# Half-width filter loads with on-chip copies, two convolutions joined without a store, and the last output blocks of a hybrid encoder layer

## The chip, the cores and the metric

The kernel runs on one core of one Trainium2 chip. The metric is the device time of one execution in microseconds (us). A core has five engines with a queue each: TensorE (PE in the profile), VectorE (DVE), ScalarE (ACT), GpSimd (POOL) and SyncE (SP), which here only issues transfers. Each engine works through its own instructions in a fixed order and waits where an operand is not there yet.

## What is computed

One encoder layer on 2048 rows of 1024 channels, in float32. The parts that matter here are the long convolutions of the Hyena group (512 channels, order 2) and the end of the layer:

```python
for o, gate in enumerate((g1, g2)):
    conv = irfft(rfft(z, n=2 * L, axis=1) * spec[:, o], n=2 * L, axis=1)[:, :L]
    z = gate * (conv + z * skip[o])
...
h = h + square(relu(rms_norm(h, norm_ff_g) @ ff_w1)) @ ff_w2
return rms_norm(h, final_norm_g)
```

Beside the Hyena group stand an mLSTM group, cross-attention and the MLP; all of them start from large projections.

## The kernel before

**The order of the program.** The projections are products of 32-bit data split into a high and a low half (`mm3`, lines 336 to 338: three matmuls per tile). While the input projection runs (`sweep`, `natural`), the filter spectra are made (`filters`) and then the two convolutions (`hyena`); `weave` alternates between the Python generators by the cost that each `yield` names, and a scheduler then sets the order on each engine by its own model of time. After that come the mLSTM scan, attention, and the MLP (`ffn`).

**A convolution** is a Fourier transform of 4096 points in two stages of small matrices. For each order `o` (0 and 1) there are three phases. *Phase 1*, 8 steps: rows of `z` are loaded (`load1`), multiplied with `f1` (L863), copied out of PSUM and stored to `zs` in device memory. *Phase 2*, 16 steps: `load2` fetches the matrices `dm` and `em`, a transposed piece `t` of `zs`, and the filter's real and imaginary parts `hr` and `hi` from `hd`. The product with `dm` (L877) is multiplied with the complex filter on ACT (L879, L880: the two halves swapped, one negated), DVE (L881, L883) and POOL (L882), multiplied with `em` (L845), copied (L846) and stored to `zg`. As real and imaginary rows lie in partitions 0 to 63 and 64 to 127, `hr` and `hi` are needed twice each, in both halves, and are loaded twice (L818, L819). *Phase 3*, 8 steps: `load3` fetches `zg` and the gate, the product with `e2` (L896) is multiplied by the gate (L897). For order 0 the result is stored to `z1` (L899), from which phase 1 of order 1 loads it again. Large tiles of the convolution share one ring of 10 buffers (`ta`), and all their transfers are issued by SP.

**The end.** The MLP's second product runs as 28 products of halves, each in two column blocks `tp` with four steps `k` (12 matmuls of 128x512 a step). In the last seven (`o == 3`) finished blocks are turned: `turn` transposes four 128x128 tiles (L1653), ACT squares and sums them (L1655), DVE multiplies by the gain (L1656). `finish` combines two halves of sums into a row scale (`rsqrt`, ten small DVE instructions), multiplies 8 tiles by it (L1671 on DVE, L1673 on ACT) and stores them (L1677). These pieces wait in the list `outs`, from which one or two are taken in each step:

```python
for _ in range(min(len(outs), 2 if len(outs) > 5 else 1)):
    outs.pop(0)("mm" if tp else "hy")
```

What is left after the last step is emitted after it: with this rule two turns of block 0, its `finish`, four turns of block 2 and its `finish`.

Of the kernel before, what the change touches and what calls it, by code (L numbers as in the profile page):

```python
# [13 lines left out]
ALU = mybir.AluOpType  # L14
# [5 lines left out]
D = 1024  # L20
CH = 512
EPS = 1e-6
# [103 lines left out]
class Prog:  # L126
# [654 lines left out]
    def hyena(self, es):  # L781
# [4 lines left out]
        z1 = self.dram("z1", (128, 16, CH))  # L786
# [15 lines left out]
        def load1(o, j2):  # L802
            z = ta()
            js = slice(2 * j2, 2 * j2 + 2)
            nc.sync.dma_start(out=z, in_=hy[0, :, js] if o == 0 else z1[:, js])
# [43 lines left out]

        for o in range(2):  # L850
            sd, gd = sds[o], gds[o]
            q = [load1(o, 0), load1(o, 1)]
            for j2 in range(8):
                yield 3.5
                js = slice(2 * j2, 2 * j2 + 2)
                z = q.pop(0)
                if j2 < 6:
                    q.append(load1(o, j2 + 2))
                st = [ta() for p in range(2)]
                for jj in range(2):  # L860
                    for p in range(2):
                        pp = self.hy()
                        nc.tensor.matmul(pp, f1[:, p], z[:, jj], start=True, stop=True)  # L863
                        self.copy(st[p][:, jj], pp)
                for p in range(2):
                    nc.sync.dma_start(out=sd[p, :, js], in_=st[p])
            nxt = load2(o, 0)
            for i in range(16):
# [5 lines left out]
                gs = ta()  # L874
                for m in range(2):
# [11 lines left out]
            for j2 in range(8):  # L887
                yield 3.5
# [22 lines left out]
                nc.sync.dma_start(out=yh[:, js], in_=sq)  # L911

# [299 lines left out]
    def attention(self, es):  # L1212
# [64 lines left out]
        for c in range(4):  # L1277
# [129 lines left out]
            def stats(c=c, ssum=ssum):  # L1407
# [12 lines left out]
                nc.vector.reciprocal(rbp[:, 4 * c:4 * c + 4], rbp[:, 4 * c:4 * c + 4])  # L1420
# [89 lines left out]
    def ffn(self):  # L1510
# [115 lines left out]
        with tc.tile_pool(name="down", bufs=1) as B:  # L1626
# [31 lines left out]
            def finish(c, dst, last):  # L1658
                rb = self.rbp[:, 4 * c:4 * c + 4]
                m = B.tile([128, 4], F32, tag="mo", name="mo", bufs=2)  # L1660
                nc.vector.tensor_tensor(m, ss[:, c, 0], ss[:, c, 1], ALU.add)
                nc.vector.tensor_tensor(m, m, rb, ALU.mult)
                nc.vector.tensor_tensor(m, m, rb, ALU.mult)
                nc.vector.tensor_scalar(m, m, 1.0 / D, EPS, ALU.mult, ALU.add)
                rv = self.rsqrt(B, m, "or")
                nc.vector.tensor_tensor(rv, rv, rb, ALU.mult)
                for h in range(2):
                    for t in range(4):
                        v = dst[h][:, t]
                        if last and t % 2:  # L1670
# [3 lines left out]
                        if last and t % 2 or t == 3:  # L1674
                            n = 2 if last else 4
                            r0 = 512 * c + 128 * (t + 1 - n)
                            nc.sync.dma_start(  # L1677
                                out=self.out[r0:r0 + 128 * n, 512 * h:512 * h + 512].rearrange("(t p) c -> p t c", p=128),
                                in_=dst[h][:, t + 1 - n:t + 1])

            def turned(c, tp, h, i, j):
                return [lambda tag, t=t: turn(c, h, acc[i, tp], acc[j, tp], t, tag) for t in range(4)]
# [8 lines left out]
            for s, (n, tp, k) in enumerate(down):  # L1691
# [19 lines left out]
                for _ in range(min(len(outs), 2 if len(outs) > 5 else 1)):  # L1711
                    outs.pop(0)("mm" if tp else "hy")
                if k < 3:
                    continue
                for m in range(4):
# [3 lines left out]
                    else:  # L1719
                        nc.vector.tensor_tensor(v, bank[m], v, ALU.add)  # L1720
# [15 lines left out]
                elif i == 3:  # L1736
# [3 lines left out]
                    outs += turned(c, tp, 0, 3, 6)  # L1740
                    outs.append(lambda tag, c=c, d=(acc[6, tp], acc[1, tp]): finish(c, d, False))
                elif i == 2:
                    outs += turned(2 * tp, tp, 0, 2, 7)
                elif i == 4:
                    outs += turned(2 * tp, tp, 1, 4, 5)
                    outs.append(lambda tag, c=2 * tp, d=(acc[7, tp], acc[5, tp]), tp=tp: finish(c, d, tp))
# [108 lines left out]
```

## Time and profile before

| | |
|---|---|
| three runs | 3331.58, 3334.69, 3346.91 us; median 3334.69 |
| profiled execution | 3330.15 us, of which the span on the core 3328.4 us |
| PE busy | 3155.0 us, 95% of the span |
| DVE, ACT, POOL busy | 1975.6, 1473.0, 1253.8 us |
| data moved | 680.87 MB, mean 205 GB/s over the span |

PE is the engine that carries the span, so the question in each stretch is where PE stands still, or runs at a lower granted clock, and what ended last before it went on. A busy share near 1 of the DMA engines in a stretch says that the transfers themselves are the limit there. PE's busy time is a model: matmuls are pipelined, and the records of one overlap with the next.

### The profile page before, as it was taken

The page shows a single profiled execution, that of the slowest core. Times are in us where ns is not written, and L with a number is a line of the kernel's source. Part 1 is how long each engine was busy: PE and PEld are TensorE (multiplying, and loading weights), DVE is VectorE, ACT ScalarE, POOL GpSimd, SP SyncE. Part 2 cuts the span into 40 slices and gives each one's busy share as a digit, 9 for nine tenths or more (in the row PEclk, how much of TensorE's full clock was granted, in tenths as well). Part 3 has the DMA queues.
Part 4 walks back from the last instruction along what each step waited for, and adds up shares of the span by engine and source line. Part 5 has one row for each costly group of instructions (what it writes and reads, how often), then busy time and mean ns, then how long its engine had stood idle before and what let it go on. Part 6 is the DMA issues. An engine that isn't in the chain of part 4 may idle for free.

```text
span 3328.4 us, 45502 instructions
## 1 busy us (share of the span) xinstructions
PE 3155.0 (95%) x15293; PEld 2512.1 (75%) x15293; DVE 1975.6 (59%) x3312; ACT 1473.0 (44%) x2827; POOL 1253.8 (38%) x868
## 2 busy tenths in 40 slices
PE   7999999899999998699999998999999999999997
PEld 5655666576666887598888897888788887888876
DVE  7684324433555755676766565665754686565695
ACT  5442444542454244355454444555655543333335
POOL 0132000220122303634334115876765574434482
PEclk9999999999999999899999999999999999999998
DMA  5553897999998669858557525764644475444434
GB/s 177 178 195 134 291 310 248 281 267 347 247 270 272 220 214 301 273 155 249 177 186 237 188 95 185 227 204 161 223 163 152 158 238 167 130 139 143 127 93 160
DMA packets 483461, 680.87 MB, mean 205 GB/s; under 512 B 40816, under 2 KB 252912, under 8 KB 482204
## 3 DMA queue, kind: packets, MB, share of 16 engines
q1 hardware_dynamic: 482584, 676.04, 64.6%
q8 instruction: 121, 1.98, 0.2%
q0 software_dynamic: 496, 1.84, 0.2%
q14 instruction: 112, 0.92, 0.1%
q10 hardware_dynamic: 148, 0.10, 0.0%
HBM read 458.64 MB, written 219.18 MB: 204 GB/s over the span
## 4 chain that ended last, share of the span: by engine, by line
PE 72%; DMA 14%; DVE 5%; issue 3%; ACT 2%; POOL 2%; SPq 1%; ACTq 0%; DVEq 0%; POOLq 0%
PE mm L336 14%; PE mm L337 14%; PE mm L338 14%; PE hy L338 5%; PE hy L336 5%; PE hy L337 5%; DMA a<-hd 2%; PE hy L271 2%; PE hy L319 2%; PE hy L896 2%; DVE wl L341 1%; DMA rw<-rows 1%; PE hy L863 1%; PE mm L719 1%; PE hy L286 1%
## 5 line engine op out<-in xcount | busy, mean ns | idle before, releaser
L341 DVE TENSOR_TENSOR wl<-wn,wh 128x512 fp32r<-128x512 f32 (+1 forms) x364 | 290.8, 836 | 152.7 <-ACT wh L341 140.5
L1436 DVE TENSOR_TENSOR bl<-wr,bh 128x512 fp32r<-128x512 f32 x213 | 239.4, 1131 | 123.9 <-ACT bh L1435 121.5
L341 ACT CAST wh<-wn 128x512 fp32r<-128x512 f32 (+1 forms) x364 | 208.4, 618 | 230.8 <-DMA wn<-in_w_in_dram 79.8
L1435 ACT CAST ah<-w 128x512 fp32r<-128x512 f32 x284 | 176.1, 621 | 298.8 <-PE hy L337 152.1
L336 PE MATMUL mm<-xh,wh 128*128 128x512 f32 x640 | 280.3, 440 | 6.5 <-ACT P L685 2.9
L337 PE MATMUL mm<-xl,wh 128*128 128x512 f32 x640 | 276.4, 433 | 0.6 <-DVE xl L498 0.6
L338 PE MATMUL mm<-xh,wl 128*128 128x512 f32 x640 | 266.3, 417 | 0.0
L882 POOL TENSOR_TENSOR b<-b,a 128x512 f32<-128x512 f32 x64 | 88.8, 1390 | 466.2 <-DVE a L823 211.5
L1436 DVE TENSOR_TENSOR al<-w,ah 128x512 fp32r<-128x512 f32 x236 | 229.2, 973 | 58.6 <-ACT ah L1435 58.3
L1435 ACT CAST bh<-wr 128x512 fp32r<-128x512 f32 x232 | 143.3, 621 | 234.1 <-PE mm L338 171.4
L338 PE MATMUL mm<-bh,al 128*128 128x512 f32 x576 | 225.6, 394 | 7.7 <-DVE al L1436 4.9
L336 PE MATMUL mm<-bh,ah 128*128 128x512 f32 x576 | 227.2, 394 | 0.0
L337 PE MATMUL mm<-bl,ah 128*128 128x512 f32 x576 | 226.0, 392 | 0.0
L336 PE MATMUL mm<-act,wh 128*128 128x512 f32 x512 | 200.0, 394 | 0.9 <-ACT wh L341 0.9
L337 PE MATMUL mm<-act,wh 128*128 128x512 f32 x512 | 200.5, 392 | 0.0
L338 PE MATMUL mm<-act,wl 128*128 128x512 f32 x512 | 198.8, 392 | 0.0
L1293 POOL TENSOR_TENSOR ssum<-ssum,sq 128x512 f32<-128x512 f32 x56 | 80.7, 1441 | 278.8 <-ACT sq L1292 278.8
L336 PE MATMUL hy<-bh,ah 128*128 128x512 f32 x448 | 175.3, 392 | 0.0
L337 PE MATMUL hy<-bl,ah 128*128 128x512 f32 x448 | 174.8, 390 | 0.0
L338 PE MATMUL hy<-bh,al 128*128 128x512 f32 x448 | 174.7, 390 | 0.0
L295 POOL TENSOR_TENSOR b<-b 128x512 f32<-128x512 f32 x32 | 66.5, 2078 | 281.8 <-DVE b L290 147.9
L336 PEld LDWEIGHTS mm<-xh,wh 128*128 128x128 f32 x640 | 122.2, 191 | 64.0 <-issue 30.0
(365 smaller groups left out, 8861.3 us busy)
## 6 DMA issues: line engine op xcount, KB each, us to landing
wr<-hc SPq DMA_DIRECT2D x224, 256.0 KB
w<-in_ff_w_dram SPq DMA_DIRECT2D x176, 256.0 KB
a<-hd SPq DMA_DIRECT2D x128, 256.0 KB
hc<-t SPq DMA_DIRECT2D x128, 256.0 KB
wn<-in_w_in_dram SPq DMA_DIRECT2D x100, 256.0 KB
hc<-q SPq DMA_DIRECT2D x96, 256.0 KB
fs<-a SPq DMA_DIRECT2D x32, 512.0 KB
a<-fs SPq DMA_DIRECT2D x32, 512.0 KB
```

What stands on the lines that cost most here:

```text
L271: nc.tensor.matmul(pp, f1[:, p], e[p], start=True, stop=True)
L295: nc.gpsimd.tensor_tensor(e[1], f, b, ALU.subtract)
L319: nc.tensor.matmul(pp, dm[:, m], t[:, m], start=True, stop=True)
L336: mm(ps, lh, rh, start=start, stop=False)
L337: mm(ps, lh, rl, start=False, stop=False)
L338: mm(ps, ll, rh, start=False, stop=stop)
L341: both = (self.nc.scalar.copy(hi, src), self.nc.vector.tensor_tensor(lo, src, hi.bitcast(F32), ALU.subtract))
L882: nc.gpsimd.tensor_tensor(xt, xt, hi[:, m], ALU.mult)
L896: nc.tensor.matmul(pp, e2[:, p], r[p][:, jj], start=p == 0, stop=p == 1)
L1293: nc.gpsimd.tensor_tensor(ssum, ssum, sq, ALU.add)
L1435: self.nc.scalar.copy(hi, src)
L1436: eng.tensor_tensor(lo, src, hi.bitcast(F32), ALU.subtract)
```

## The change

There are four parts.

1. `load2` loads `hr` into partitions 0 to 63 and `hi` into 64 to 127 only. A new function `double` makes the other halves on the chip: ACT copies `hr` upward, DVE copies `hi` downward, 64 partitions by 1024 numbers each. For the first piece one row is set apart as before, now without a transfer.
2. Phase 3 of order 0 and phase 1 of order 1 are one loop. The gated result stays on the chip, and the function `spectrum` (phase 1 in a form for both orders) multiplies it with `f1` one step later; `z1` is gone. A step of this loop names a cost of 7.0 and no longer 3.5.
3. In the last product two pieces of `outs` are taken in each step, and `finish` is part of its block's last turn, so block 0 is done within the last product and only block 2 is left after it. All stores go out in pieces of 256 rows by 512 columns; most are issued by ACT, the others by SP. In blocks 0 and 2 one half is multiplied on DVE.
4. The row scale is worked out with fewer small instructions: `rbp` holds EPS times the square of the mean square, and `finish` needs two instructions ahead of `rsqrt` and none behind it.

```diff
         def load2(o, i):
...
-            for h in range(2):
-                nc.sync.dma_start(out=hr[64 * h:64 * h + 64], in_=src[0])
-                nc.sync.dma_start(out=hi[64 * h:64 * h + 64], in_=src[1])
+            nc.sync.dma_start(out=hr[0:64], in_=src[0])
+            nc.sync.dma_start(out=hi[64:128], in_=src[1])
+            return dm, em, t, hr, hi
+
+        def double(i, hr, hi):
+            nc.scalar.copy(hr[64:128], hr[0:64])
             if i == 0:
-                nc.sync.dma_start(out=hr[64:65, 0], in_=hd[o, 0, 64:65])
-                nc.vector.memset(hi[0:1, 0], 0.0)
+                nc.scalar.copy(hr[64:65, 0], hi[64:65, 0])
                 nc.vector.memset(hi[64:65, 0], 0.0)
-            return dm, em, t, hr, hi
+            nc.vector.tensor_copy(hi[0:64], hi[64:128])
...
+        def spectrum(o, j2, z):
+            st = [ta() for p in range(2)]
+            for jj in range(2):
+                for p in range(2):
+                    pp = self.hy()
+                    nc.tensor.matmul(pp, f1[:, p], z[:, jj], start=True, stop=True)
+                    self.copy(st[p][:, jj], pp)
+            for p in range(2):
+                nc.sync.dma_start(out=sds[o][p, :, 2 * j2:2 * j2 + 2], in_=st[p])
...
                 if i < 15:
                     nxt = load2(o, i + 1)
                 gs = ta()
+                double(i, hr, hi)
...
             for j2 in range(8):
-                yield 3.5
+                yield 3.5 if o else 7.0
...
                 if o == 0:
-                    nc.sync.dma_start(out=z1[:, js], in_=gate)
+                    late(lambda j2=j2, gate=gate: spectrum(1, j2, gate))
                     continue
...
+            late(None)
...
-                nc.vector.reciprocal(rbp[:, 4 * c:4 * c + 4], rbp[:, 4 * c:4 * c + 4])
+                nc.vector.scalar_tensor_tensor(rbp[:, 4 * c:4 * c + 4], rbp[:, 4 * c:4 * c + 4], EPS,
+                                               rbp[:, 4 * c:4 * c + 4], ALU.mult, ALU.mult)
...
-            def finish(c, dst, last):
-                rb = self.rbp[:, 4 * c:4 * c + 4]
+            def finish(c, dst):
                 m = B.tile([128, 4], F32, tag="mo", name="mo", bufs=2)
-                nc.vector.tensor_tensor(m, ss[:, c, 0], ss[:, c, 1], ALU.add)
-                nc.vector.tensor_tensor(m, m, rb, ALU.mult)
-                nc.vector.tensor_tensor(m, m, rb, ALU.mult)
-                nc.vector.tensor_scalar(m, m, 1.0 / D, EPS, ALU.mult, ALU.add)
+                q = self.rbp[:, 4 * c:4 * c + 4]
+                for h in range(2):
+                    nc.vector.scalar_tensor_tensor(m, ss[:, c, h], 1.0 / D, m if h else q, ALU.mult, ALU.add)
                 rv = self.rsqrt(B, m, "or")
-                nc.vector.tensor_tensor(rv, rv, rb, ALU.mult)
-                for h in range(2):
-                    for t in range(4):
+                for t in range(4):
+                    for h in range(2):
                         v = dst[h][:, t]
-                        if last and t % 2:
+                        if h and c % 2 == 0:
                             nc.vector.tensor_scalar(v, v, rv[:, t:t + 1], None, ALU.mult)
                         else:
                             nc.scalar.mul(v, v, rv[:, t:t + 1])
...
+                        if t % 2:
+                            r0 = 512 * c + 128 * (t - 1)
+                            (nc.sync if h and c % 2 == 0 else nc.scalar).dma_start(
...
-                for _ in range(min(len(outs), 2 if len(outs) > 5 else 1)):
+                for _ in range(min(len(outs), 2 if len(outs) > 4 or n + 1 == len(prods) else 1)):
                     outs.pop(0)("mm" if tp else "hy")
...
-                        nc.vector.tensor_tensor(v, bank[m], v, ALU.add)
+                        d = nc.vector.tensor_tensor(v, bank[m], v, ALU.add)
+                        if s + 1 == len(down):
+                            tc.keep_in_program_order(d)
```

The number of matmuls is the same. The order of the instructions differs in the convolutions' stretch and at the end; between them and ahead of them it is the same but for a few neighbours that changed places. Three places show it.

SP, phase 2 of order 0, the loads of one step: before, with `zs0` the transformed signal, `hd` the filter, `em` and `dm` the matrices and `zg0` the result.

```order
L815 DMA a_3907<-zs0_3223 128x2x512
L818 DMA a_3908<-hd_321 64x2x512
L819 DMA a_3909<-hd_321 64x2x512
L813 DMA em_3904<-in_c_em_dram 128x256
L818 DMA a_3908<-hd_321 64x2x512
L819 DMA a_3909<-hd_321 64x2x512
L848 DMA zg0_3225<-a_3821 128x2x512
L812 DMA dm_3973<-in_c_dm_dram 128x256
```

And the same step of the changed kernel on SP.

```order
L814 DMA a_3903<-zs0_3222 128x2x512
L816 DMA a_3904<-hd_321 64x2x512
L817 DMA a_3905<-hd_321 64x2x512
L812 DMA em_3900<-in_c_em_dram 128x256
L849 DMA zg0_3224<-a_3813 128x2x512
L811 DMA dm_3969<-in_c_dm_dram 128x256
```

Two of eight transfers of a step are gone; the others stand in the same order.

ACT in the same step: before, `b` is the swapped product, `P` a piece of the input projection that leaves PSUM, `a_3821` the result on its way to `zg`.

```order
L846 COPY a_3821<-hy_3840 128x512
L879 ACTIVATE b_3918<-hy_3916 64x512
L880 COPY b_3918<-hy_3916 64x512
L846 COPY a_3821<-hy_3925 128x512
L879 ACTIVATE b_3931<-hy_3929 64x512
L880 COPY b_3931<-hy_3929 64x512
L685 COPY P_4378<-mm_4487 128x512
```

And the changed kernel on ACT, where `a_3904` is the `hr` of the step after.

```order
L847 COPY a_3813<-hy_3836 128x512
L882 ACTIVATE b_3914<-hy_3912 64x512
L883 COPY b_3914<-hy_3912 64x512
L685 COPY P_4441<-mm_4416 128x512
L821 COPY a_3904<-a_3904 64x1024
L847 COPY a_3813<-hy_3921 128x512
L882 ACTIVATE b_3927<-hy_3925 64x512
L883 COPY b_3927<-hy_3925 64x512
L847 COPY a_3909<-hy_3934 128x512
```

The copy of `hr` stands between the other work of ACT, five instructions ahead of the step that uses it.

ACT at the end of the program, from the squares of the last turns on (`ss` the sums, `or_y` the row scale, `acc` the output tiles): before.

```order
L1655 ACTIVATE junk_29702,ss_24134<-mm_29697 128x512
L1655 ACTIVATE junk_29710,ss_24134<-mm_29705 128x512
L1655 ACTIVATE junk_29718,ss_24134<-mm_29713 128x512
L1655 ACTIVATE junk_29726,ss_24134<-mm_29721 128x512
L1673 ACTIVATE acc_24122<-acc_24122,or_y_29674 128x512 x4
L1673 ACTIVATE acc_24126<-acc_24126,or_y_29674 128x512 x4
L1673 ACTIVATE acc_24123<-acc_24123,or_y_29734 128x512 x2
L1673 ACTIVATE acc_24127<-acc_24127,or_y_29734 128x512 x2
```

And the changed kernel on ACT at its end.

```order
L1675 ACTIVATE acc_24095<-acc_24095,or_y_29615 128x512 x4
L1678 DMA out_0_dram<-acc_24095 128x2x512 x2
L1660 ACTIVATE junk_29672,ss_24107<-mm_29667 128x512
L1660 ACTIVATE junk_29680,ss_24107<-mm_29675 128x512
L1660 ACTIVATE junk_29688,ss_24107<-mm_29683 128x512
L1660 ACTIVATE junk_29696,ss_24107<-mm_29691 128x512
L1675 ACTIVATE acc_24096<-acc_24096,or_y_29702 128x512 x4
L1678 DMA out_0_dram<-acc_24096 128x2x512 x2
```

The multiplications of block 0 (four on ACT, `acc_24095`) and their stores now stand ahead of the squares of block 2; behind those, ACT has four multiplications and not twelve.

More of the change, by code (lines that the diff above doesn't have):

```diff
@@ L848, in back @@
                 nc.sync.dma_start(out=dst.rearrange("(k r) j c -> (r j) k c", k=2), in_=gs)
-        for o in range(2):
-            sd, gd = sds[o], gds[o]
-            q = [load1(o, 0), load1(o, 1)]
-            for j2 in range(8):
-                yield 3.5
[L855 to L866, printed above, removed]
+        def spectrum(o, j2, z):
[7 more added lines that the diff above has]
+                nc.sync.dma_start(out=sds[o][p, :, 2 * j2:2 * j2 + 2], in_=st[p])
+        q = [load1(0), load1(1)]
+        for j2 in range(8):
+            yield 3.5
+            if j2 < 6:
+                q.append(load1(j2 + 2))
+            spectrum(0, j2, q.pop(0))
+        for o in range(2):
+            gd = gds[o]
             nxt = load2(o, 0)
@@ L1673, in finish, with turned, one @@
                             nc.scalar.mul(v, v, rv[:, t:t + 1])
[L1674 to L1682, printed above, removed]
+                        if t % 2:
+                            r0 = 512 * c + 128 * (t - 1)
+                            (nc.sync if h and c % 2 == 0 else nc.scalar).dma_start(
+                                out=self.out[r0:r0 + 256, 512 * h:512 * h + 512].rearrange("(t p) c -> p t c", p=128),
+                                in_=dst[h][:, t - 1:t + 1])
+            def turned(c, tp, h, i, j, dst=None):
+                def one(tag, t):
+                    turn(c, h, acc[i, tp], acc[j, tp], t, tag)
+                    if dst and t == 3:
+                        finish(c, dst)
+                return [lambda tag, t=t: one(tag, t) for t in range(4)]
             def add(i, j, tp, eng):
```

12 lines of the change are left out of this document (4 added, 8 removed).

## Prediction

> **What bounds the kernel now.** I read the page first, then the table of windows, the waits and the chain of waits in the convolutions' stretch, and last the timeline of the end. The page's first part says which engine carries the span (busy us, share, instructions).
>
> ```profile
> PE 3155.0 (95%) x15293; PEld 2512.1 (75%) x15293; DVE 1975.6 (59%) x3312; ACT 1473.0 (44%) x2827; POOL 1253.8 (38%) x868
> ```
>
> PE is busy for 95%, so a change that keeps all its matmuls can win only where PE stands still or runs slowly. The change touches two places: the convolutions (490 to 1150 us) and the last 40 us. The table of windows cuts the first by phase: phase 2 of order 0, then phases 3 and 1, then phase 2 of order 1. Behind the length stand the busy times of PE, PEld, DVE, ACT and POOL, the granted clock, the DMA share and GB/s.
>
> ```profile
> 560.00:740.00 180.00, 158.87 (x747) 116.11 (x746) 79.58 (x122) 89.30 (x156) 42.88 (x32) 0.96 1.01 267
> 740.00:860.00 120.00, 120.00 (x590) 85.09 (x589) 50.75 (x74) 30.82 (x57) 0.00 (x0) 1.00 0.90 326
> 860.00:1050.00 190.00, 174.40 (x666) 120.59 (x665) 99.67 (x139) 102.85 (x164) 45.88 (x32) 0.97 0.98 258
> ```
>
> In the two phases 2 PE idles 180 - 158.9 = 21.1 and 190 - 174.4 = 15.6 us, while the DMA engines are busy all the time (1.01 and 0.98). Between them PE has no gap. The clock takes more: 4% of 158.9 and 3% of 174.4 are 6.4 and 5.2 us. So 36.7 us of idling and 11.6 us of slow clock, 48.3 together, are all that the convolutions can return. That transfers are the cause is seen in the chain of waits of the first window, and in the longest waits for transfers between 490 and 1150 us (total, times, longest):
>
> ```profile
> by line: DMA a<-hd 33.2%; DMA zg<-a 12.8%; DMA a<-zs 7.5%; PE mm L336 5.2%; PE mm L337 5.1%; PE mm L338 5.0%; DMA em<-in_c_em_dram 4.6%; PE hy L877 4.0%; DMA wn<-in_w_in_dram 3.9%; PE hy L845 3.6%; DMA kn<-st 3.4%; DMA dm<-in_c_dm_dram 3.3%
> ACT wh L341 <- DMA wn<-in_w_in_dram: 57.9, 13, 8.4
> ...
> POOL b L882 <- DMA a<-hd: 45.2, 7, 12.2
> ...
> DVE b L881 <- DMA a<-hd: 31.0, 7, 6.5
> ```
>
> A third of the chain is the load that the change halves, and the projection's weights `wn` come late in the same crowd.
>
> **The change part by part.** *Half the filter loads.* The DMA view has the counts and sizes; its packet lines for the two phases 2 have their traffic.
>
> ```profile
> a<-hd SPq DMA_DIRECT2D x128, 256.0 KB
> ...
> z<-a SPq DMA_DIRECT2D x8, 512.0 KB
> a<-z SPq DMA_DIRECT2D x8, 512.0 KB
> DMA packets 34438, 48.09 MB, mean 267 GB/s; under 512 B 3923, under 2 KB 17982, under 8 KB 34426
> DMA packets 34356, 48.94 MB, mean 258 GB/s; under 512 B 2677, under 2 KB 17340, under 8 KB 34343
> ```
>
> 64 of 128 loads go, 32 in each order: 32 x 262 KB = 8.4 MB. Order 0 keeps 48.1 - 8.4 = 39.7 MB, at its 267 GB/s 149 us; PE needs 158.9 - 6.4 = 152.5 us at full clock. Order 1 keeps 40.5 MB, at 258 GB/s 157 us, against 174.4 - 5.2 = 169.2 us of PE. In both the transfers fall below PE, in order 0 only just. Requests come in bursts, so not every gap closes. I let order 0 end at 161 us (19 less, two thirds of 21.1 + 6.4) and order 1 at 176 (14 less, two thirds of 15.6 + 5.2): **33 us**. The lower bound is zero (the gaps stay and fall to the next wait), the upper 48.3. On SP the 64 issues free time too, but nothing on PE waits for that by itself.
>
> *The copies.* The nearest rows for 64x1024 numbers from SBUF to SBUF are these (busy us, mean ns of one):
>
> ```profile
> L341 ACT CAST xh<-xt 128x1024 fp32r<-128x1024 f32 x8 | 8.4, 1050 | 10.1 <-DVE xt L461 10.1
> L706 DVE TENSOR_SCALAR cv<-cv 128x1040 f32<-128x1040 f32 x4 | 2.8, 696 | 0.0
> ```
>
> 32 x 1.05 = 33.6 us on ACT and 32 x 0.70 = 22.4 us on DVE, over 370 us in which ACT works 89.3 + 102.9 and DVE 79.6 + 99.7. They are hidden beside that as long as the half-load has landed when the copy's turn comes. If not, all that is queued behind the copy waits: on ACT the exits of the projection from PSUM (L685) and the swapped halves (L879, L880), on DVE L881 and L883, and PE behind both. If every copy lay on the path it would be 33.6 + 22.4 = 56 us; below nothing it cannot go. Of the two ends I stand near the first, since the scheduler put the copy a few instructions ahead of its user and the loads now come sooner: I charge **4 us**, a tenth of a microsecond for each of the 64 copies with some for late ones.
>
> Here a mechanism on POOL is to be weighed. The lists of L882 and L883 show their durations (shortest, median, longest ns):
>
> ```profile
> L882 POOL TENSOR_TENSOR b<-b,a x64: 1261/1292/2252, 564.5 to 1043.1; 128x512 f32<-128x512 f32 x64
> L883 DVE TENSOR_TENSOR b<-b x64: 678/693/1816, 572.0 to 1044.4; 128x512 f32<-128x512 f32 x64
> ```
>
> A few of these take about one operation of the other engine longer (2252 - 1292 = 960 ns, 1816 - 693 = 1123). The Trainium skill says why, in "SBUF — State Buffer", section "Who interferes with whom": DVE and GpSimd share a pair of ports as an exclusive lock, and a copy in a 2-port mode holds it to its end. By that rule each DVE copy can hold up POOL; the medians show that it is the exception for the pair above. It is a rival below.
>
> *The join.* 16 transfers of 512 KB go (8.4 MB), and one trip through device memory. In 740 to 860 us PE had 120.00 of 120 us, so this hides nothing that costs and I cost it at nothing. What can go wrong: a step takes five tiles of the ring of ten where it took three, and SP waits at the gate's load for a tile that `spectrum` frees one step earlier; behind it stand the weights `wn`. If each of 8 steps lost a load of some 5 us, 40 us would go. The named cost of 7.0 leaves a step about twice the time, so I take 0.
>
> *The end.* The row of the chain that follows PE's last product, then rows of the timeline, then three of the last windows of 2 us:
>
> ```profile
> 3305.34 0.45 PE mm L1653 x4
> 3304.00 2.47 DVE L1720 TENSOR_TENSOR acc<-hy,acc 128x512 f32<-128x512 f32 x4
> ...
> 3308.41 0.60 ACT L1655 ACTIVATE junk<-mm 128x512 f32<-128x512 f32 x1
> ...
> 3309.13 0.60 ACT L1655 ACTIVATE junk<-mm 128x512 f32<-128x512 f32 x1
> 3309.13 0.69 DVE L1656 TENSOR_TENSOR acc<-mm,gl 128x512 f32<-128x512 f32 x1
> ...
> 3312.31 7.45 ACT L1673 ACTIVATE acc<-acc,or_y 128x512 f32<-128x512 f32 x12 [2.49 <-DVE or_y L1666]
> ...
> 3313.22 0.16 DVE L1666 TENSOR_TENSOR or_y<-or_y,rbp 128x4 f32<-128x4 f32 x1
> 3313.41 1.67 DVE L1671 TENSOR_SCALAR acc<-acc,or_y 128x512 f32<-128x512 f32 x4
> 3314.89 7.43 SPq L1677 DMA_DIRECT2D out_dram<-acc  x6
> 3314.00:3316.00 2.00, 0.00 (x0) 0.00 (x0) 1.09 (x3) 2.00 (x5) 0.00 (x0) 0.50 0.10 38
> 3316.00:3318.00 2.00, 0.00 (x0) 0.00 (x0) 0.00 (x0) 2.00 (x5) 0.00 (x0) 0.50 1.02 381
> ...
> 3326.00:3328.00 2.00, 0.00 (x0) 0.00 (x0) 0.00 (x0) 0.00 (x0) 0.00 (x0) 0.50 0.44 163
> ```
>
> PE's last product ends at E = 3305.3, the span 23.1 us later. Two blocks are finished in that time, 4.2 MB; at 381 GB/s their stores take 11 us, from about 3315.8 to 3326.9 by the shares of the windows. Afterwards only block 2 is left, 2.1 MB or 5.5 us. Its path from E, an estimate from these rows: DVE first has block 0's four multiplications (1.67), for which it must wait some time, then the four sums (2.47), and is done at about E + 3.0 where it was E + 1.1; the turns and four squares, one each 0.72 us (3308.41 to 3309.13), to E + 6.6; the last gain (0.69) and eleven small DVE instructions, one each 0.2 us (3313.22 to 3313.41), to E + 9.5; two multiplications and the issue to E + 10.4; transfers begin 0.9 us after the issue, as now (3314.89 to 3315.8), run 5.5 us, and the span ends 1.5 us after the last, as now: E + 18.3. That saves 23.1 - 18.3 = 4.8 us; four transposes of block 0 now stand ahead of E and cost 0.45. **4 us**, between 1 (ACT's issues of stores delay the casts `bh` ahead of PE) and 7 (block 0's multiplications find a gap). The fewer small instructions of the other `finish` calls lie beside a busy PE: nothing.
>
> *The sum* against the profiled execution (3330.15 us; 1.75 of it outside the span): -33 + 4 - 4 = -33, so 3297. The median of the three runs, 3334.69, is 4.5 above that execution; I let medians lie half of that above, the start at 3332.4, and predict **3300 us**.
>
> **The rivals.** *The gaps stay.* Transfers leave, but PE's gaps were ended by ACT and DVE, and these still wait for `wn` and `zs`. For it: PE itself hardly waits for a transfer, and ACT's 57.9 us for `wn` are more than either wait for `hd`. Against it: the share of 1.0 in both windows. Then only a quarter of 48.3 returns, 12, and 4 at the end; the copies still cost 4: 3332.4 - 12 - 4 + 4 = 3320.
>
> *Ports.* Each DVE copy holds up POOL or waits for it, up to 0.70 us a step on the chain L882, L883, L845: 32 x 0.70 = 22 us. Against it: POOL works 42.9 of 180 us. It would be -33 + 4 + 22 - 4 = -11: 3321. This is what the lock on the page named above would do here.
>
> *Slower: the copy of `hr` blocks ACT.* ACT takes its instructions in order. Where the copy waits for its load, L685 cannot empty the projection's four PSUM banks and PE stops. Before, only DVE and POOL waited for `hd`, 31.0 and 45.2 us. It decides where the load lands after the copy's turn in most steps; then the 56 us lie on the path, half of the 33 is lost, and the end gives 4: 56 - 16 - 4 = +36, some 3368. Against it: DVE also empties banks and also waited, and the load comes sooner than now.
>
> **How the numbers follow.** No change is taken as within 0.5%, 16.7 us, about what a measurement of this kernel can tell: 3318 to 3351. Forecast 0.75; the gaps stay 0.09; ports 0.04; slower 0.12. The forecast lies below 3318 as long as 15 of its 33 us are there. So faster 0.75, same 0.13, slower 0.12. The range: downward all 48.3 with 3 us at the end and no cost of copies would be about 3281; I take 3283. Upward both middle rivals (3320, 3321) with some room, 3326. Outside remain the slow rival and a little more.
>
> **What would show it.** Right: in the windows of the two phases 2 PE idles under 12 us together at a clock near 1.0, the DMA share is below 1 in order 1, ACT's waits for `hd` at the copy are a few us, and the span ends about 18 us after PE's last product. Wrong: the windows keep their 180 and 190 us; a wait of ACT's copy for `hd` is the longest in the stretch and PE waits for L685 behind it; POOL's L882 has a median far above 1.3 us; or PE gets gaps where phases 3 and 1 are joined, with SP waiting at the gate's load.

## The result and the profile after

| | before | after |
|---|---|---|
| median of 12 runs | 3338.69 us (3327.43 to 3348.42) | 3339.28 us (3330.56 to 3345.46) |
| ratio of after to before | | 0.9998, 95% interval 0.9985 to 1.001 |
| profiled execution | 3330.15 us | 3338.86 us |

The change moves the time by nothing that can be measured. The forecast was 3300 us, with a range of 3283 to 3326: it is wrong. One caution for the two traces: the profiled execution of before lies 8.5 us below that kernel's median, the one of after at its median, so 9 us between their spans is scatter, not the change. Much of it lies where the two kernels hardly differ: from the 6500th matmul to the last product the trace of before takes 1820 us, that of after 1826, and all others from 1822 to 1832.

The first part of the page of after: PE's work is the same; DVE works 11.1 and ACT 32.6 us longer, mostly through the copies.

```profile
PE 3157.4 (95%) x15293; PEld 2513.5 (75%) x15293; DVE 1986.7 (60%) x3334; ACT 1505.6 (45%) x2857; POOL 1252.6 (38%) x868
```

The same three windows of the convolutions as before: length, busy PE, PEld, DVE, ACT, POOL, granted clock, DMA share, GB/s.

```profile
560.00:740.00 180.00, 164.66 (x775) 118.66 (x773) 90.17 (x140) 109.29 (x176) 42.47 (x32) 0.96 0.81 236
740.00:860.00 120.00, 119.98 (x585) 85.52 (x584) 51.99 (x78) 33.75 (x58) 0.00 (x0) 1.00 0.71 239
860.00:1050.00 190.00, 177.77 (x679) 123.43 (x678) 106.87 (x150) 118.29 (x179) 44.97 (x32) 0.97 0.76 213
```

The transfers did fall away: the DMA share is 0.81 and 0.76 where it was 1.01 and 0.98. But PE still idles 15.3 and 12.2 us (21.1 and 15.6 before), and the clock stays at 0.96 and 0.97. What it waits for is seen in the waits of engines between 490 and 1150 us, and in those of SP, which issues the transfers, in the windows of order 0 and order 1 (one row each).

```profile
ACT a L821 <- DMA a<-hd: 92.4, 27, 6.7
DVE a L825 <- DMA a<-hd: 70.7, 25, 5.9
...
ACT wh L341 <- DMA wn<-in_w_in_dram: 9.9, 6, 3.0
```

```profile
SPq L849 <- ACT a L847: 32.9, 11, 6.9
SPq L849 <- ACT a L847: 46.0, 11, 10.2
```

The weights `wn`, ACT's worst wait before (57.9 us), are on time now. In their place both copies wait for `hd`: L821 on ACT 27 times, L825 on DVE 25 times, 163 us together. One such place, from the timelines of ACT, DVE, POOL and PE (start, us, idle time before and what ended it):

```profile
1029.80 1.04 ACT L821 COPY a<-a 64x1024 f32<-64x1024 f32 x1 [3.98 <-DMA a<-hd]
1030.87 0.58 ACT L847 COPY a<-hy 128x512 f32<-128x512 f32 x1
1031.48 0.59 ACT L882 ACTIVATE b<-hy 64x512 f32<-64x512 f32 x1
1032.09 0.58 ACT L883 COPY b<-hy 64x512 f32<-64x512 f32 x1
1030.45 0.69 DVE L825 COPY a<-a 64x1024 f32<-64x1024 f32 x1 [3.25 <-DMA a<-hd]
1032.74 1.27 POOL L885 TENSOR_TENSOR b<-b,a 128x512 f32<-128x512 f32 x1 [6.27 <-ACT b L883]
1034.04 0.69 DVE L886 TENSOR_TENSOR b<-b 128x512 f32<-128x512 f32 x1 [0.65 <-POOL b L885]
1034.88 1.10 PE L846 MATMUL hy<-b,em 128*128 128x512 f32 x2 [2.57 <-DVE b L886]
```

ACT stands 3.98 us at the copy for a load. Behind it wait the exit of an earlier step (L847) and the swapped halves (L882, L883) of a product that belongs to the step before, has nothing to do with that load and left PE at about 1026.9 us; POOL waits 6.27 us for these, DVE for POOL, and PE 2.57 us for DVE. ACT takes its instructions in order: the Trainium skill says the same in "PSUM — Partial Sum Buffer", section "Engine vs sequencer instructions" (the queues of ScalarE, VectorE and GpSimd are strict FIFOs), and these rows agree.

For the comparison of versions the program is cut by matmuls, of which each version has 15293: a first stretch from the end of the 1500th to that of the 5500th (the convolutions and what follows to the scan), a second to the 6500th (the mLSTM scan beside attention). Before, then after, in the columns of the windows:

```profile
439.10:1283.00 843.90, 791.51 (x4003) 599.12 (x4002) 420.17 (x798) 352.05 (x603) 142.60 (x107) 0.98 0.89 267
1283.00:1485.80 202.80, 162.45 (x1002) 145.13 (x1001) 122.77 (x286) 92.13 (x278) 103.66 (x78) 0.90 0.78 238
440.90:1276.80 835.90, 792.86 (x4001) 598.79 (x4001) 439.47 (x826) 387.18 (x637) 143.58 (x106) 0.98 0.77 240
1276.80:1493.10 216.30, 163.27 (x1003) 146.71 (x1002) 119.69 (x289) 92.09 (x280) 102.66 (x78) 0.87 0.73 225
```

The first stretch wins 8 us and the second loses 13.5 us, some 11 of which show again in the runs below. At the end, the last product of after, its last multiplications and the last windows:

```profile
3318.29 0.39 PE L338 MATMUL hy<-bh,al 128*128 128x512 f32 x1
3327.60 1.67 DVE L1673 TENSOR_SCALAR acc<-acc,or_y 128x512 f32<-128x512 f32 x4
3330.00:3332.00 2.00, 0.00 (x0) 0.00 (x0) 0.00 (x0) 0.16 (x1) 0.00 (x0) 0.50 1.02 367
...
3334.00:3336.00 2.00, 0.00 (x0) 0.00 (x0) 0.00 (x0) 0.00 (x0) 0.00 (x0) 0.50 0.50 185
```

PE's last product ends at 3318.7, the span at 3337.2: 18.5 us, where it was 23.1.

### The profile page after: what moved, and what is told of

The parts are those of the page before. It is cut to its first block, busy times and chain, and to the rows that moved or that the text cites. A ratio compares the mean times of both kernels' runs of the same rounds, so it can differ in the third digit from the quotient of the medians.

```text
span 3337.2 us, 45444 instructions
## 1 busy us (share of the span) xinstructions
PE 3157.4 (95%) x15293; PEld 2513.5 (75%) x15293; DVE 1986.7 (60%) x3334; ACT 1505.6 (45%) x2857; POOL 1252.6 (38%) x868
## 4 chain that ended last, share of the span: by engine, by line
PE 74%; DMA 10%; DVE 6%; issue 4%; ACT 3%; POOL 1%; SPq 1%; DVEq 0%; ACTq 0%; POOLq 0%
PE mm L336 15%; PE mm L337 15%; PE mm L338 15%; PE hy L336 5%; PE hy L338 5%; PE hy L337 5%; PE hy L271 2%; PE hy L856 2%; PE hy L319 2%; DMA a<-hd 1%; PE hy L899 1%; DMA rw<-rows 1%; DVE bl L1441 1%; DVE wl L341 1%; PE hy L286 1%
## 5 line engine op out<-in xcount | busy, mean ns | idle before, releaser
L885 POOL TENSOR_TENSOR b<-b,a 128x512 f32<-128x512 f32 x64 | 87.4, 1366 | 461.5 <-ACT b L883 420.8
```

The costliest lines, as they stand in the source:

```text
L885: nc.gpsimd.tensor_tensor(xt, xt, hi[:, m], ALU.mult)
```

## The experiments

Each ratio is to the kernel before, with its 95% interval; 0.01 is 33 us. Lines quoted are the two stretches of that version's profile.

**Each half of the change alone (e1, e2).** e1 is the kernel before with parts 1 and 2 of the diff, e2 with parts 3 and 4.

> The kernel before with the convolutions' parts of the change alone (half loads, copies, joined loop); end and row scales as before. In the two traces that are there PE's idle time up to the 4500th matmul went from 39 to 34 us only, and the last store ends 15 us after PE's last matmul instead of 20. Theory A (the convolutions return some 3 us, the end 5, and later stretches differ by scatter between executions): 3 us less than before, 3333 to 3338. Theory C (the new order in the convolutions costs the later stretches, 1283 to 1460 us above all, what it gained): 0 to 6 us more than before. The prediction's sum would have -29.

> The kernel before with the changes of the last product and of the row scales alone. The prediction's term: 4 us less than before (1 to 7). Theory A agrees: -5. If the term is only moved to another place (DVE's multiplications delay PE before its last product, 1.2 us lost there in the trace after): 0 to -3.

Measured: e1 1.0022 (1.0007 to 1.0036), 7 us slower than before; e2 0.9987 (0.9976 to 0.9998), 4 us faster. e1 went the way of theory C, a little beyond its 0 to 6 us.

```profile
437.90:1273.00 835.10, 789.11 (x4003) 595.60 (x4002) 438.03 (x826) 386.83 (x637) 143.70 (x106) 0.99 0.77 240
1273.00:1488.90 215.90, 165.44 (x1003) 149.17 (x1002) 121.32 (x291) 92.94 (x281) 102.25 (x78) 0.87 0.74 227
438.40:1285.00 846.60, 793.85 (x4003) 599.20 (x4002) 417.65 (x797) 351.97 (x603) 144.81 (x106) 0.98 0.88 266
1285.00:1491.40 206.40, 162.20 (x1003) 145.33 (x1002) 123.78 (x287) 91.64 (x279) 103.92 (x78) 0.88 0.77 237
```

The stretches repeat: 835 and 216 us with the convolutions changed, 847 and 206 without (844 and 203 in the trace of before).

**Nobody waits for the filter (e3, e4).** In both, the two products read a constant tile, so that the filter is left out of the result:

```diff
-nc.vector.tensor_tensor(y, pp, hr[:, m], ALU.mult)
-nc.gpsimd.tensor_tensor(xt, xt, hi[:, m], ALU.mult)
+nc.vector.tensor_tensor(y, pp, one, ALU.mult)
+nc.gpsimd.tensor_tensor(xt, xt, one, ALU.mult)
```

e3 is the changed kernel with this edit and without `double`; e4 is the kernel before with this edit and all its loads.

> The changed kernel with the half loads still made, but without the copies, and with the two products by the filter multiplied by a constant tile of ones instead: so the convolution's result leaves the filter out, no engine waits for the filter's loads, and the traffic is that of the changed kernel. Theory A (PE's remaining gaps come from ACT's and DVE's copies, which wait 92 and 71 us for the loads and hold all that is queued behind them): PE idles under 15 us up to the 4500th matmul, and the time is 15 to 30 us below the changed kernel. Rival B (the gaps were ended by the weights, the state's transposes and zs and stay): 0 to 8 us below it.

> The kernel before with all four quarter loads of the filter still made, but the filter's two products multiplied by a constant tile of ones: the filter is left out of the result, nobody waits for its loads, the traffic stays (share of the DMA engines about 1 in both phases 2). If bandwidth was the limit, as the prediction read the share of 1.0: PE still idles 30 us or more up to the 4500th matmul, through weights and zs, and the time is within 8 us of before. If waiting for the filter itself was: 15 us or more below before.

Measured: e3 0.9889 (0.9874 to 0.9904), 36 us below the changed kernel; e4 1.0009 (0.9995 to 1.0024), no change. So before was held by the transfers themselves: with four loads a step it is as slow when nobody waits for them. And half the loads, without the copies, do bring the relief: against e2, which differs by the convolutions alone, 0.0098 or 33 us.

```profile
438.70:1242.00 803.30, 783.66 (x4003) 596.66 (x4002) 412.69 (x794) 354.63 (x603) 142.86 (x106) 0.99 0.79 249
1242.00:1458.00 216.00, 168.98 (x1003) 153.20 (x1002) 121.27 (x290) 92.01 (x279) 102.03 (x78) 0.85 0.74 226
```

**Waiting without copying, copying without waiting (e5, e6).** In e5 each load fills all partitions of one piece, both products of a step read that piece (so half of the filter is left out), and `double` is gone; in e6 the products read the constant tile as in e3, and the copies run on tiles that nothing else writes. These are the main lines of the two edits.

```diff
 # e5
-nc.sync.dma_start(out=hr[0:64], in_=src[0])
-nc.sync.dma_start(out=hi[64:128], in_=src[1])
+nc.sync.dma_start(out=hr[:, 0], in_=hd[o, 2 * i])
+nc.sync.dma_start(out=hi[:, 0], in_=hd[o, 2 * i + 1])
 # e6
-nc.scalar.copy(hr[64:128], hr[0:64])
-nc.vector.tensor_copy(hi[0:64], hi[64:128])
+for m in range(2):
+    nc.scalar.copy(ca[64:128], ca[0:64])
+    nc.vector.tensor_copy(cd[0:64], cd[64:128])
```

> The changed kernel without copies but with the waits for the loads: each of the two half loads now fills all 128 partitions of one 512-wide piece, and both products of a step read it, so half of the filter is left out of the result; traffic and number of loads as in the changed kernel. Theory A1 (the copies' place is the cost: they stand early in ACT's and DVE's queues and hold everything behind them until the load lands): without them the time comes near the run that waits for nothing, 3303 to 3312. Rival A2 (any wait for the filter, wherever it stands, costs this, since the loads land late): 3320 to 3340.

> The run that waited for no filter load (products by ones, so the filter is left out), with the copies' work put back: in each step ACT copies twice 64x512 numbers within a tile that nothing else writes, DVE too, and no copy waits for a load. Theory A (waiting, not copying, costs): within 6 us of that run, 3300 to 3309. Rival (the 56 us of copying lie on the path, the upper end of the prediction's bound): 3330 or more; half of it 3318.

Measured: e5 0.9864 (0.9842 to 0.9886), e6 0.9887 (0.9865 to 0.9909). e6 equals e3, so the work of the copies, here two of half the size for each, costs nothing that can be measured. In e5 the products take the loads themselves, and the only wait for `hd` left is one of DVE, 2.2 us. Only the two together cost: a copy that waits, in a place where other work queues behind it. Against e5 the changed kernel loses 0.0134 or 45 us, against e3 36.

```profile
441.60:1236.30 794.70, 780.57 (x4003) 593.92 (x4002) 411.84 (x792) 354.31 (x603) 143.44 (x106) 1.00 0.75 251
439.20:1242.00 802.80, 781.08 (x4002) 593.26 (x4002) 439.15 (x859) 393.48 (x667) 144.39 (x106) 1.00 0.78 249
```

So the loads land in time for the products, and not for copies that stand further ahead. In the order of ACT shown ahead of the prediction the copy stands five rows ahead of the halves of its own step; between them lie the exits of two steps and the swapped halves of a product of the step before. Over all 32 copies of the changed kernel it is 3 to 11 rows, 7 in the median. That is half a step to a whole step of work. Why the scheduler puts it there is not shown; e7 fits that it takes the load as landed too soon.

**Loads earlier, copies elsewhere (e7, e8).** `loadh` issues `hr` and `hi` two steps ahead; in e8 both copies are `nc.gpsimd.tensor_copy` too.

```diff
-sb.tile([128, 2, CH], F32, tag="a", name="a", bufs=10)
+sb.tile([128, 2, CH], F32, tag="a", name="a", bufs=11)
...
+fil = [loadh(o, 0), loadh(o, 1)]
...
+if i < 14:
+    fil.append(loadh(o, i + 2))
```

> The whole computation: the changed kernel with the half loads issued two steps ahead instead of one, in a ring of 11 tiles instead of 10. Theory A: the waits of ACT's and DVE's copies for the loads fall from 92 and 71 us to under 30 each, PE's idle time up to the 4500th matmul from 34 to some 15 us, and the time by 15 to 25 us, to 3315 to 3325. Rival (SP holds the loads back, behind stores that wait for ACT, however early they are named): within 6 us of the changed kernel.

> The whole computation: loads two steps ahead and a ring of 11 as in the run before, and both copies on POOL instead of ACT and DVE. Also, by the order of its instructions, the stretch from 1283 to 1460 us stands on PE as in the kernel before, and on DVE and ACT nearly so. Theory A: no copy holds ACT or DVE, some 25 us less than the changed kernel, and if the order costs the 11 us of the stretch from the 5500th to the 6500th matmul, that stretch takes 203 to 206 us instead of 216: together 3305 to 3315. Rival (POOL is too slow for two copies a step, or takes the port that DVE needs): DVE waits for POOL, 3330 to 3345.

Measured: e7 0.9976 (0.996 to 0.9991), its waits at the copies 86.9 and 75.7 us: a miss for theory A. The order fits that: with the loads a step earlier the copies were drawn forward as well. ACT's copy now stands 10 to 24 rows ahead of the halves that it goes with, 17 in the median, where that of the changed kernel stood 7. e8 0.9926 (0.9906 to 0.9946), 25 us below before: in both phases 2 POOL has little but this chain to do, and copies that wait there (L825 120.9 us for `hd`, 59.4 of them once) hold up little else. The price of a copy on POOL is seen in e17 below.

**Copies late (e9, e10).** The same copies, pinned (written out here without the functions around them and without the row set apart in the first piece); e10 has the early loads of e7 too:

```diff
 nc.scalar.copy(xt[64:128], pp[0:64])
+if m == 0:
+    tc.keep_in_program_order(nc.scalar.copy(hr[64:128], hr[0:64]))
 nc.vector.tensor_tensor(y, pp, hr[:, m], ALU.mult)
+if m == 0:
+    tc.keep_in_program_order(nc.vector.tensor_copy(hi[0:64], hi[64:128]))
```

> The whole computation; against the changed kernel only the places of the copies differ: the copy of hr is pinned behind the first swapped halves of its own step on ACT, the copy of hi behind the first product with hr on DVE. In the changed kernel the scheduler had drawn ACT's copy half a step to a whole step ahead of its users. Same copies, same loads. Theory A1 (the copy's early place is the cost): ACT's wait for hd at the copy falls from 92 us to under 30, the stretch from the 1500th to the 4500th matmul from 698 to some 665 us, and the time to 3300 to 3312. Rival (the loads land too late for the users as well): within 10 us of the changed kernel.

> The whole computation: copies pinned as in the run before, and the half loads issued two steps ahead in a ring of 11. Theory A1: no copy waits for a load any more, under 10 us in all, and 0 to 8 us below the run before. On PE the stretch from 1283 to 1460 us has the order of the kernel before here; if that order is what costs the later stretch its 11 us, the 5500th to 6500th matmul take 203 to 206 us instead of 216.

The figures of 655 to 702 us that the expectations here and below give for the stretch from the 1500th to the 4500th matmul are the time of the 4500th from the span's start (698 in after); the stretch itself took 258 us there. So read, e9 came to 665, e12 to 708, e17 to 665 and e18 to 683.

Measured: e9 0.9986 (0.9973 to 1.0), e10 0.9963 (0.9949 to 0.9976), 12 us below before. ACT no longer waits for `hd` at the copy, and PE's idle time in the first stretch falls from 43 us (835.9 - 792.9, after) to 27 (e9). But the second stretch takes 235 us in both:

```profile
439.30:1254.90 815.60, 788.53 (x4002) 599.75 (x4002) 446.25 (x803) 392.37 (x648) 133.89 (x99) 0.99 0.76 243
1254.90:1490.50 235.60, 166.03 (x1002) 148.51 (x1002) 126.67 (x309) 84.71 (x266) 109.44 (x85) 0.84 0.72 217
```

Part of it is shifted work (309 DVE instructions there instead of 289), so for e8, e9, e10, e15 and e16 only the sum of both stretches may be compared: e9 1051, e10 1045, e8 1027, after 1052, before 1047. What e9 won it lost at once, and why is open. The expectation of e10 that PE's own order decides the second stretch also fell.

**Join and halves apart (e11, e12).** e11 is the changed kernel with the loads of before and no `double`, e12 the one with separate loops.

> The changed kernel with full loads of the filter and no copies, so with the joined loop and the end alone. In the stretch from 1283 to 1460 us its instructions stand nearly as before on all engines (10 and 9 rows of DVE and ACT differ, none of PE). Prediction's step: the join costs and brings nothing; the end 5 us: 3331 to 3336, and the stretch from the 5500th to the 6500th matmul takes 203 to 207 us. If the stretch's 11 us come from the join's freed traffic or its five tiles: 213 or more there.

> The changed kernel without the joined loop: half loads, copies and end alone. Theory A: the copies' waits eat the loads' relief without the join too, so the stretch from the 1500th to the 4500th matmul takes 695 to 702 us, and the time is 3333 to 3342. If the join is what spoilt it: 15 us or more below that.

Measured: e11 0.9999 (0.9984 to 1.0014), e12 1.0004 (0.9991 to 1.0017). e12 shows that halves, copies and the end bring nothing without the join either. e11 keeps the order of before behind the convolutions, and its second stretch takes 206 us:

```profile
442.00:1294.20 852.20, 792.78 (x4003) 597.88 (x4002) 414.59 (x796) 352.71 (x603) 144.18 (x106) 0.98 0.86 255
1294.20:1500.30 206.10, 162.93 (x1001) 146.34 (x1001) 122.58 (x285) 91.03 (x277) 103.25 (x78) 0.88 0.77 235
```

So with the order of before, or nearly, that stretch took 203, 206, 204 and 206 us (before, e2, e4, e11); with that of the changed kernel, or nearly, 216, 216, 216, 213, 218 and 217 (after, e1, e3, e5, e6, e7), though the convolutions ended up to 40 us earlier in some of these. This points to how the scan's instructions stand, not to when it starts. e12, whose order is neither of the two, took 211 us. But e8 and e10, with half loads and, on PE, the order of before from about the 5720th matmul on, took 219 and 235 us, shifted work included: PE's order alone is not it. No run put the order of before on all engines behind half loads, so this cause is argued from the groups, not isolated.

**The scan's load of og (e13 to e16).** In the changed kernel SP waits longer for POOL, which frees the only buffer of `og`. In the order of SP its load stands ahead of two loads of `rw` now, behind which it stood before (before, then after):

```order
L1067 DMA kk_t_11988<-kt_75 128x4x128
L1067 DMA rw_11644<-rows_9097 128x512
L1067 DMA rw_11646<-rows_9097 128x512
L1030 DMA og_11535<-od_78 128x512
```

```order
L1071 DMA kk_t_11961<-kt_75 128x4x128
L1034 DMA og_11508<-od_78 128x512
L1071 DMA rw_11617<-rows_9070 128x512
L1071 DMA rw_11619<-rows_9070 128x512
```

The waits of SP at it in the second stretch of before, after and e9:

```profile
SPq L1030 <- POOL ht L1147: 9.3, 4, 4.6
SPq L1034 <- POOL ht L1151: 23.9, 5, 7.9
SPq L1040 <- POOL ht L1157: 33.7, 6, 7.7
```

```diff
-og = load(n, "og", od, 1)
+og = sb.tile([128, 4, 128], F32, tag="og", name="og", bufs=1)
+nc.gpsimd.dma_start(out=og.rearrange("p h d -> p (h d)"), in_=od[:, n])
```

> The changed kernel with one difference behind the convolutions: the load of og in the mLSTM scan, whose only buffer is freed by POOL, is issued by POOL and no longer by SP. Theory D (the 11 us lost between the 5500th and the 6500th matmul are SP's waits for POOL at that load, 24 us against 9 before, with the scan's other loads queued behind): the stretch falls from 216 to 203 to 208 us and the time by 8 to 12 us, to 3327 to 3331. Rival (the order of other engines, or the transfers themselves): 213 or more, within 4 us of the changed kernel.

> The kernel before with the load of og issued by POOL. Theory D: SP waited 9 us there, so the stretch falls by 0 to 8 us from 203 to 206, and the time by as much. Rival: no change or slower, since POOL is held while it issues.

> The whole computation: copies pinned behind their step's first halves, half loads two steps early, ring of 11, and og loaded by POOL. Without the last this version took 235 us from the 5500th to the 6500th matmul, SP waiting 34 us for POOL at og in the version with the loads one step early. Theory D: that stretch falls to 205 to 215 us and the time by 20 to 30 us, to 3297 to 3307. Rival: within 8 us of 3327.

> The whole computation: both copies on POOL, half loads two steps early, ring of 11, and og loaded by POOL. Without the last 3314 and 219 us in the stretch. Theory D: 205 to 212 there, and 3300 to 3307 in all. Rival: within 4 us of 3314.

Measured: e13 0.9992 (0.998 to 1.0004), e14 1.0016 (0.9999 to 1.0032), e15 0.9986 (0.9972 to 0.9999), e16 0.9959 (0.9946 to 0.9972). With `og` off SP the second stretch takes 209 us in the changed kernel (e13, from 216) and 209 in the one before (e14, from 203): the difference between the two vanishes, but through a loss of before as much as through a gain of the changed kernel. The changed kernel's time fell by 2 us, which the intervals do not tell from nothing, where 8 to 12 were expected. With the other orders `og` off SP made the sum of both stretches longer: from 1045 to 1053 us in e15 (against e10), from 1027 to 1034 in e16 (against e8). So the load explains the difference between before and after at most in part, and theory D does not hold for the other orders.

**The cause by itself (e17, e18).** e17: the loops apart as in e12, the copy of `hr` pinned late on ACT as in e9, that of `hi` late on POOL; behind the convolutions the order is nearly the changed kernel's. e18: the store of `zg` issued by `nc.scalar`.

> The whole computation: the loops not joined, half loads, the end as changed; the copy of hr on ACT pinned behind the first swapped halves of its own step, the copy of hi on POOL, pinned ahead of its first user there. Behind the convolutions the order of the instructions is the changed kernel's but for 26 rows of SP, 2 of DVE and 5 of ACT. Theory A1: the stretch from the 1500th to the 4500th matmul takes 655 to 667 us, and with the same order the one from the 5500th to the 6500th takes 213 to 218; so the gain is kept, and the time is 3298 to 3308. Rival (late copies only move the time to a later stretch, as the earlier run's 3336 would say): 3325 to 3340.

> The changed kernel with the store of zg issued by ACT, right behind the copy that it waits for, instead of by SP. SP waited 79 us for ACT at that store in both phases 2, with the next step's loads behind it. If that loop (load, copy, store, next load) sets the pace: ACT's and DVE's waits for hd fall below half of 92 and 71 us, the stretch from the 1500th to the 4500th matmul takes 665 to 680 us, and the time is 15 to 30 us below the changed kernel. If the copies' early place alone costs: within 6 us of the changed kernel.

Measured: e17 0.9936 (0.9919 to 0.9953), 3317 us, 21 us below before. No wait of ACT for `hd` is left; POOL waits 16 us for it. The order of ACT, one step, with the copy directly behind the halves of the product that uses it:

```order
L884 ACTIVATE b_4392<-hy_4390 64x512
L885 COPY b_4392<-hy_4390 64x512
L822 COPY a_4317<-a_4317 64x1024
```

POOL's copies (shortest, median, longest ns) and the two stretches:

```profile
L829 POOL COPY a<-a x32: 1032/1367/2062, 570.9 to 1002.2; 64x1024 f32<-64x1024 f32 x32
440.30:1253.50 813.20, 783.38 (x4001) 595.74 (x4001) 422.37 (x788) 389.88 (x642) 184.60 (x137) 0.99 0.81 256
1253.50:1467.80 214.30, 160.85 (x1002) 144.74 (x1001) 120.68 (x295) 91.46 (x278) 103.92 (x79) 0.86 0.75 231
```

The first stretch is 23 us shorter than in the changed kernel, the second the same: with the order behind it kept, late copies win and keep what they win. The closest pair is e12 and e17, which differ only in where the copies stand and in the engine of the one of `hi`. The two stretches of e12:

```profile
439.60:1283.80 844.20, 796.25 (x4001) 600.50 (x4001) 438.57 (x824) 386.59 (x637) 143.40 (x106) 0.98 0.78 247
1283.80:1495.10 211.30, 168.07 (x1003) 150.95 (x1002) 121.65 (x291) 92.02 (x281) 103.29 (x78) 0.87 0.77 232
```

The copies' place alone is worth 0.0068 or 23 us. It does not return all: e17 stays 16 us above e3 and some 10 above what was expected. At the 4500th matmul it is 33 us ahead of the changed kernel, at the 5500th 23. DVE waits 44.1 us for the late copy on ACT; whether that is where the 10 us go is open.

e18 0.9987 (0.9973 to 1.0): ACT's wait for `hd` is still 74.6 us and the first stretch 831 us. So the store's wait on SP is not the main cause; that it follows from the held ACT is the likelier reading, not shown by itself.

e8 and e17 both beat the kernel before and the changed one; their intervals overlap.

## Why the prediction was wrong

- **Half the loads, -33 us: right.** The DMA share fell below PE as worked out, and without the copies the runs gave 33 us (e3 against e2) and 41 (e5 against e2). Within the 33 the first stretch won 43 us (847 to 803) and the second gave 10 back, which the step did not have: that both make just 33 is luck.
- **The copies, +4 us: this is the step that failed.** They cost 36 us (the changed kernel against e3; 45 against e5), between the bounds 0 and 56. The failed sentence is that "the scheduler put the copy a few instructions ahead of its user and the loads now come sooner": these few instructions, 7 in the median, were work of the step before, and the loads did not come soon enough for that: ACT waited 92.4 and DVE 70.7 us for them. Their work is free (e6); the queue behind a waiting copy is not (e5, e8, e17).
- **The slower rival had the mechanism,** ACT's queue behind the copy, at a chance of 0.12. Its price of 56 was too high, and it took half of the relief away on top. The measured terms, -33 + 36 - 4, add up to the measured change of -0.7 us but for rounding. That is no test: each is the difference of two neighbours in the row before, e2, e3, after.
- **The gaps stay:** PE's gaps mostly stayed, as this rival said (15.3 and 12.2 us of 21.1 and 15.6), but not through `wn` (57.9 to 9.9 us). Its time of 3320 was wrong.
- **Ports: did not happen.** L885 on POOL has a median of 1282 ns (L882 before: 1292). The lock that the Trainium skill describes in "SBUF — State Buffer", section "Who interferes with whom", had hardly an occasion: two of the 32 DVE copies began while L885 ran on POOL, and just these two were long, 858 and 1716 ns, where the other 30 took 689 to 692. So the trace agrees with the lock, and the chain seldom brings the two together.
- **The join, 0 us: not contradicted.** e11 and e2 differ by 4 us, after and e12 by 2 the other way. In the first stretch the pairs point opposite ways (852 to 847, 836 to 844), so its share there stays open.
- **The end, -4 us: right.** 18.5 us behind the last product, as against the 18.3 worked out; -4.3 us measured alone (e2).
- **Not foreseen:** the order behind the convolutions. The text ahead of the prediction called it the same but for a few neighbours. On PE, ACT, DVE, POOL and SP the scan's stretch did stand otherwise (28 of POOL's 78 instructions there, for one), and with it went some 11 us. On SP the load of `og`, for one, moved ahead of two loads of `rw`. What in that order costs is open: taking `og` off SP removed the difference in one pair of kernels and made others slower.

## What to carry to other kernels

Traffic saved by work on the chip is worth what the profile says only if the new work does not wait in a queue that others need: look where the scheduler puts it and how many rows lie between it and its user, not only how long it takes. A copy that must wait for a load goes right ahead of its user, or to an engine with little else to do (e17 and e8; in e9 what that won was lost again behind it). After such a change look at later stretches by themselves, since a scheduler may set them in another order. And count the rows over all steps: the one step shown ahead of the prediction had five, where the median was 7 and the largest 11.

## What the runs showed of the hardware

A copy of 64x1024 numbers within SBUF took 690 ns on DVE and 1046 ns on ACT (medians in the changed kernel), and 1034 to 1367 ns on POOL (medians in e8 and e17). Where PE had nearly no gaps the granted clock was full: with 0.65 us idle in the window from 560 to 740 us (e5) it was 1.00. With 15.3 us idle there it was 0.96 (after), but with 16.6 us 0.99 (e1), so the idle time alone does not set it.

```profile
560.00:740.00 180.00, 179.35 (x875) 130.12 (x874) 85.85 (x133) 96.18 (x166) 42.47 (x32) 1.00 0.83 281
```
